# A whole decoder layer on eight cores: longest path first in the kernel's static scheduler, gated first transfers, and a first FFN group by token-block pairs

## The chip, the cores and the metric

The kernel runs on the 8 cores of one Trainium2 chip. Each core computes one sequence of the batch, with no traffic between cores. The metric is the device time of the slowest core, in microseconds (us). Most executions agree within 0.3%. In some executions one die (cores 0 to 3 or 4 to 7) gets a lower TensorE clock and the time is some per cent longer; those are called slow, and only fast runs are compared here.

## The reference, cut to what matters

One decoder layer on x (8, 2048, 1024) float32, with D = 1024 and a feed-forward width of 2816:

```python
x = x + 0.5 * swiglu(rmsnorm(x, ffn1_norm), w1, w3, w2)       # first FFN
h = rmsnorm(x, mix_norm)
u = h @ w_in                                                  # q, k, v, g_ret, x_lru, g_lru
ret   = retention_chunkwise(rotary(q), rotary(k), v)          # mixer A, 4 heads, 16 chunks of 128
y_ret = (silu(g_ret) * head_groupnorm(ret)) @ w_ret_o
xc    = causal_depthwise_conv(x_lru)                          # mixer B, 4 taps
r, i  = sigmoid(xc @ w_r + b_r), sigmoid(xc @ w_i + b_i)      # 8 blocks of 128 channels
a     = exp(-8 * r * softplus(-lam))
h_t   = a * h_{t-1} + sqrt(1 - a*a) * (i * xc)                # RG-LRU, a scan over time
y_lru = (h_t * gelu(g_lru)) @ w_lru_o
# ... sigmoid gates merge the two, then cross-attention on 256 memory tokens,
# the second FFN and the last rmsnorm
```

Retention and the RG-LRU (called the LRU from here) read the same `h` and do not depend on each other. The stretch of time in which both run is called the mixer.

## The kernel before

The kernel records every operation with what it reads and writes, its engine and a modelled cost. A scheduler in the same file then simulates the engines once, at build time, and fixes the order of every engine's queue. On the chip each queue runs in that order: an instruction whose data are late holds everything behind it on its engine (41.30 us of POOL in `norm_inline` below). So a modelled cost never delays anything on the chip by itself; it acts only by the order that it produces. Among the operations that its simulation holds to be ready, the scheduler takes the smallest `key`, and `key` is the place in the program.

```python
DMA_NS_PER_B = 1.0 / 300.0      # modelled DMA rate: 300 bytes per ns
DMA_LAT = 2000.0
TAB_NS = 1283.0                 # modelled load of an activation table
TAB_HOLD = 1200.0               # extra reluctance to change the table
...
        op.key = op.id if key is None else key     # program order
...
            if op.dma:
                s2 = max(end, dmafree[0])
                dmafree[0] = s2 + op.dma * DMA_NS_PER_B
                end = dmafree[0] + DMA_LAT         # when the scheduler believes the data have landed
```

The start: x comes as sixteen tiles of 128 tokens, each normalised (ACT square, POOL power, DVE scale), transposed by PE (8 small matmuls) and copied out. The FFN's weights come in blocks on another queue. All sixteen tiles stand in the program ahead of the first projection.

```python
    row = load_row("ffn1_norm", 0)
    consts_early()
    for tt in range(4):
        load_x(tt)
    f1.pump(3)                  # weight blocks
    for tt in range(4, 8):
        load_x(tt)
    f1.pump(6)
    for tt in range(8, 16):
        load_x(tt)
    for tt in range(16):
        norm_x(tt, row, bkT)    # normalise and transpose
    f1.pump()
    consts_late()
```

The mixer is recorded as sixteen LRU units (a channel block is two units, one for each half of the sequence) alternating with sixteen retention steps. One LRU unit, cut:

```python
            # PE: input projections -> ACT copies them to XL
            dve(...tensor_scalar(xc, XL, ...))                  # conv, then 3 scalar_tensor_tensor taps
            pool(...tensor_copy(xcb, xc))                       # XCB, bf16 for PE
            # PE: gate matmuls on XCB -> ACT: tanh -> TR, TI
            dve(...scalar_tensor_tensor(ti, ti, 1.0, xc, add, mult))
            act(mu, tr, Exp); act(tr, tr, Exp); act(mu, mu, Ln); act(mu, mu, Exp)
            pool(...tensor_tensor(mu, ti, mu, mult))
            dve(...tensor_tensor_scan(xc, tr, mu, ...))
            pool(...tensor_tensor(bt, xc, gg, mult))            # BT, the unit's output
```

Retention's matmuls use PSUM banks 2, 3 (projections q, k, v, gate: `bkp`), 5, 6, 7 (its memory work: `bkm`) and 4. Its output tile is `ATOK`.

The softmax here doesn't subtract the row's maximum and nothing guards it: scores larger than these inputs give would overflow.

Of the kernel before, what the change touches and what calls it, by code (L numbers as in the profile page):

```python
# [20 lines left out]
DMA_NS_PER_B = 1.0 / 300.0  # L21
DMA_LAT = 2000.0
TAB_NS = 1283.0
TAB_HOLD = 1200.0
# [11 lines left out]
class Op:  # L36
    __slots__ = ("eng", "fn", "id", "deps", "raw", "cost", "tab", "dma", "succ", "nd", "ready", "fin",
                 "pos", "marked", "idx", "sem", "semval", "prev", "clock", "key")


class Prog:
# [27 lines left out]
    def schedule(self):  # L69
# [5 lines left out]
        for op in ops:  # L75
            for d in op.deps:
                d.succ.append(op)
        pend = {e: [] for e in ENGS}
# [47 lines left out]
        while left:  # L126
# [36 lines left out]
            op.fin = end  # L163
            op.pos = len(order[se])
# [178 lines left out]
D = 1024  # L343
KC = 8
TB = 512
NTB = 4
# [47 lines left out]
def build(stage=None):  # L394
# [135 lines left out]
    def sp_dma(out, in_, reads, writes, nbytes):  # L530
        P.add("sp", lambda e: e.dma_start(out=out, in_=in_), reads=reads, writes=writes, cost=60, dma=nbytes)  # L531

    def wdma(out, in_, reads, writes, nbytes):
        P.add("pool", lambda e: e.dma_start(out=out, in_=in_), reads=reads, writes=writes, cost=900, dma=nbytes)  # L534
# [15 lines left out]
    def load_x(tt):  # L550
        v = xt(tt)
        sp_dma(v.ap, x_d[tt * 128:(tt + 1) * 128, :], [], v.hs, 128 * D * 4)
# [3 lines left out]
    def load_row(name, slot):  # L556
        v = ROW.v(slot * D, D)
        r = ROWIDX[name]
        sp_dma(v.ap, bass.AP(rows_d.tensor, r * D, [[0, 128], [1, D]]), [], v.hs, 128 * D * 4)
        return v  # L560
# [8 lines left out]
    def consts_late():  # L569
        dve(lambda e: e.memset(onesb.ap, 1.0), [], onesb.hs, 128)  # L570
        dve(lambda e: e.tensor_scalar(maskf.ap, io_i.ap, 0.0, None, ALU.is_ge), io_i.hs, maskf.hs, 128)
        sp_dma(pc.ap, prm_d, [], pc.hs, 128 * NPCOL * 4)
# [72 lines left out]
    def norm_T(src, row, j, dst_ap, dst_hs, bk):  # L645
# [19 lines left out]
        else:  # L665
            dve(lambda e: e.tensor_copy(dst_ap, src_v), [hbk[b]], dst_hs, D)
# [15 lines left out]
    class FFN:  # L682
# [6 lines left out]
        def pump(self, upto=NM):  # L689
            while True:  # L690
# [3 lines left out]
                if ok0 and (a <= b or not ok1):  # L694
                    v = W13.v((a % 9) * 2048, 2048)
                    wdma(v.ap, w13_d[self.which][a], [], v.hs, 128 * 2048 * 4)
                    self.nl[0] += 1
                elif ok1:
                    v = W2.v((b % 9) * 1024, 1024)
                    wdma(v.ap, w2_d[self.which][b], [], v.hs, 128 * 1024 * 4)  # L700
                    self.nl[1] += 1
# [40 lines left out]
        def run(self, bkp, bk2, post, side=None, pre=None):  # L742
            side = side or []
            pre = pre or (lambda tb: None)
            m0 = 0
            pend = None
            for g, G in enumerate(GROUPS):
                ms = list(range(m0, m0 + G))
                last = g == len(GROUPS) - 1
                for tb in range(NTB):  # L750
                    if g == 0:
                        pre(tb)
                    for gm, m in enumerate(ms):
                        self.w13(m, gm, tb, G, bkp)
                        if tb == NTB - 1:
# [4 lines left out]
                    if pend is not None:  # L760
                        pms, ptb, plast = pend
                        self.w2(pms, ptb, bk2, post if plast else None)
                        if ptb == NTB - 1:
                            self.used[1] += len(pms)
                            self.pump()
                    pend = (ms, tb, last)
                m0 += G
            pms, ptb, plast = pend
            self.w2(pms, ptb, bk2, post)
# [6 lines left out]
    def mem_jobs():  # L776
# [4 lines left out]
        def jn(mt):  # L781
            def f():
                if mt == 0:
                    row[0] = load_row("mem_norm", 1)
                s = MST.v(0, D)
                sp_dma(s.ap, mem_d[mt * 128:(mt + 1) * 128, :], [], s.hs, 128 * D * 4)
# [5 lines left out]
        def jproj(src_d, dst, fp):  # L792
            def f():
                b = bk_side.next()
                for j in range(2):
                    fc = 2 * fp + j
                    w = XW.v(j * D, KC, 128)
                    wdma(XW.v(j * D, D).ap, src_d[fc], [], w.hs, 128 * D * 4)
# [102 lines left out]
    def lru_units():  # L901
# [9 lines left out]
        def unit(u):  # L911
# [41 lines left out]
            dve(lambda e: e.scalar_tensor_tensor(ti.ap, ti.ap, 1.0, xc.ap, ALU.add, ALU.mult), ti.hs + xc.hs, ti.hs, 1024)  # L953
# [4 lines left out]
            pool(lambda e: e.tensor_tensor(mu.ap, ti.ap, mu.ap, ALU.mult), ti.hs + mu.hs, mu.hs, pool_cost(1024))  # L958
# [19 lines left out]
    def ret_steps():  # L978
        bkp = Banks([2, 3])
        bkm = Banks([5, 6, 7])  # L980
# [419 lines left out]
```

## Time and profile before

| | before |
|---|---|
| time, median of 4 runs (range; 2185.85 is a slow run) | 2070.54 us (2067.56 to 2185.85) |
| span of the profiled core | 2068.1 us |
| busy share PE, DVE, ACT, POOL | 86%, 44%, 30%, 19% |
| first conv of the LRU starts | 611.7 us |
| last retention output (ATOK) ends | 1016.9 us |
| last LRU output (BT) ends | 1201.3 us |
| from there to the end | 866.8 us |

Engines in the lines below: PE is the matmul engine, PEld its weight loads, DVE, ACT and POOL the vector, scalar and general engines.

The table of windows of the kernel before. Columns: window, its length, busy us of PE, PEld, DVE, ACT and POOL (instructions), granted PE clock, DMA share, GB/s.

```profile
core 5: us, PE busy (x) PEld busy (x) DVE busy (x) ACT busy (x) POOL busy (x), PEclk, DMA share, GB/s
...
40.00:60.00 20.00, 4.25 (x40) 3.25 (x40) 6.91 (x13) 7.99 (x15) 3.13 (x4) 0.56 1.03 232
60.00:80.00 20.00, 7.00 (x40) 4.15 (x40) 6.65 (x10) 5.78 (x10) 3.25 (x5) 0.59 0.99 206
...
612.00:1010.00 398.00, 309.75 (x1506) 142.71 (x1504) 259.44 (x426) 187.22 (x314) 166.25 (x124) 0.89 0.08 19
1010.00:1201.00 191.00, 90.97 (x323) 33.89 (x322) 71.03 (x55) 94.02 (x108) 52.72 (x32) 0.70 0.12 27
1201.00:2068.00 867.00, 850.02 (x4119) 388.80 (x4116) 325.43 (x469) 204.92 (x327) 101.66 (x143) 1.00 0.24 52
```

Three stretches can be seen. At the start PE hardly works while the DMA engines are full. From 1010 to 1201 us PE is busy less than half of the time, at a granted clock of 0.70. After 1201 us PE is busy 98% of the time.

The timeline of PE at the start. Columns: start, length, engine, line, operation, output and inputs, count; in brackets the idle time before it and what ended it.

```profile
36.80 1.89 PE L505 MATMUL bank<-hT,W_45 128*128 128x512 bf16 x8
...
51.60 1.01 PE L658 MATMUL bank<-identb,HB 128*128 128x128 bf16 x8 [9.57 <-DVE HB L650]
...
67.11 1.01 PE L658 MATMUL bank<-identb,HB 128*128 128x128 bf16 x8 [7.36 <-DVE HB L650]
...
73.94 3.16 PE L505 MATMUL bank<-hT,W_45 128*128 128x512 bf16 x8
84.51 1.01 PE L658 MATMUL bank<-identb,HB 128*128 128x128 bf16 x8 [7.41 <-DVE cst L590]
85.32 4.90 PE L505 MATMUL bank<-hT,W_45 128*128 128x512 bf16 x11
```

The rows with `identb` are transposes of x tiles, the rows with `W_45` projections. Between 38.7 and 73.9 us PE does no projection, although much of it could have run (`no_gates_no_pairs` below, whose loads land at nearly the same times, runs 64 matmuls from 30 us on): its queue has the transposes of the next tiles first, and those wait for x tiles that land one about every 4 us (the sixteen transfers land from 8.3 to 68.6 us). The last wait, of 7.41 us, is of the same kind but not for an x tile: ACT stood before the square of a memory tile (`MST`, for the cross-attention), and DVE's norm of the last x tile stood behind that. ACT's timeline:

```profile
81.06 1.06 ACT L521 ACTIVATE JUNK<-MST 128x1024 bf16<-128x1024 f32 x1 [8.07 <-DMA MST<-mem]
```

PE has finished only 24 projection matmuls when its steady work begins at 85.3 us.

The chain of waits of PE from 612 to 1183 us (what it waited for, us in total, times, longest), and three lines of POOL's timeline:

```profile
PE bank L505 <- POOL XCB L939: 62.8, 8, 20.4
PE bank L505 <- DVE T_87 L1000: 38.6, 15, 4.1
PE bank L505 <- ACT TI L521: 22.6, 8, 17.5
```

```profile
1015.47 1.45 POOL L1027 TENSOR_TENSOR ATOK<-RN,SG 128x512 bf16<-128x512 f32 x1
1032.98 2.36 POOL L966 TENSOR_TENSOR BT_73<-XC,GG 128x1024 bf16<-128x1024 f32 x1 [2.60 <-DVE XC L961]
1046.97 2.35 POOL L966 TENSOR_TENSOR BT_73<-XC,GG 128x1024 bf16<-128x1024 f32 x1 [2.60 <-DVE XC L963]
```

When the last retention output is written, only four of the eight LRU channels are done; BT_73 is the fifth. The other four run alone, and the wait for XCB, up to 20.4 us at a time, is PE waiting for the LRU's next conv with nothing else in hand.

### The profile page before, as it was taken

The numbers are of one execution on the slowest core, as the hardware profiler recorded it, in microseconds if no ns is written. First come the engines' busy times: TensorE is split into PE (matmuls) and PEld (weight loads), VectorE is DVE, ScalarE is ACT, GpSimd is POOL, SyncE is SP. The second block draws the span as 40 slices with busy tenths as digits, with TensorE's granted clock in tenths as the row PEclk, the third lists the DMA queues.
The fourth block names the chain that finished last, engine by engine and source line by source line (L and its number), as shares of the span: only waits on it lengthen the run. The fifth ranks groups of instructions, "written<-read, shape, count | busy, mean of one in ns | idle before, by whom it ended". The sixth has DMA issues, their size and how long they took to land.

```text
span 2068.1 us, 24090 instructions; the slowest of 8 cores (2053.9 to 2068.1 us)
## 1 busy us (share of the span) xinstructions
PE 1776.2 (86%) x8584; PEld 815.4 (39%) x8584; DVE 904.4 (44%) x1354; ACT 615.8 (30%) x964; POOL 395.7 (19%) x435
## 2 busy tenths in 40 slices
PE   2599999999988877777554499999999999999997
PEld 1244544444443333333221144444445444444443
DVE  3445223333576657565533321115555223333346
ACT  3311121111335353535444431113544111111122
POOL 4101101000124344444322232222001000000001
PEclk9699999999998989889766799999999999999999
DMA  9706557312551010000200052218202131031013
GB/s 221 158 13 93 73 89 117 67 25 32 129 146 24 9 31 11 21 20 12 72 11 0 11 82 41 41 31 219 62 1 33 30 61 32 1 61 31 11 46 123
DMA packets 39284, 118.51 MB, mean 57 GB/s; under 512 B 4480, under 2 KB 4480, under 8 KB 38912
## 3 DMA queue, kind: packets, MB, share of 16 engines
q0 software_dynamic: 23760, 64.50, 19.6%
q1 hardware_dynamic: 15408, 52.48, 7.5%
q8 instruction: 71, 1.16, 0.2%
q14 instruction: 45, 0.37, 0.1%
HBM read 158.38 MB, written 23.07 MB: 88 GB/s over the span
## 4 chain that ended last, share of the span: by engine, by line
PE 70%; DVE 8%; DMA 6%; ACT 6%; issue 5%; POOL 2%; SPq 2%; DVEq 0%; ACTq 0%; POOLq 0%
PE bank L505 68%; DMA MST<-mem 2%; SPq L531 2%; ACT MU L521 2%; DVE XC L936 1%; ACT TR L521 1%; DMA XW<-w_xo 1%; POOL MU L958 1%; ACT L521 1%; DVE XC L933 1%; DMA X<-park 1%; PE bank L658 1%; DVE XC L963 1%; DMA XW<-w_xqT 1%; DMA rope<-RT 1%
## 5 line engine op out<-in xcount | busy, mean ns | idle before, releaser
L505 PE MATMUL bank<-hT,W_45 128*128 128x512 bf16 x2816 | 626.4, 382 | 2.3 <-ACT STMP L521 2.3
L505 PEld LDWEIGHTS bank<-hT,W_45 128*128 128x128 bf16 x2816 | 277.0, 99 | 333.4 <-issue 12.5
L505 PE MATMUL bank<-W_46,HID 128*128 128x512 bf16 x1408 | 314.2, 379 | 3.2 <-DVE stat L641 1.8
L719 DVE TENSOR_TENSOR HID<-bank,STMP 128x512 bf16<-128x512 f32 x176 | 121.7, 691 | 440.8 <-PE bank L505 439.1
L521 ACT ACTIVATE STMP<-bank 128x512 f32<-128x512 f32 x176 | 104.8, 596 | 686.0 <-PE bank L505 685.9
L737 DVE SCALAR_TENSOR_TENSOR X<-bank,X 128x512 f32<-128x512 f32 x256 | 176.2, 691 | 111.6 <-PE bank L505 111.3
L505 PEld LDWEIGHTS bank<-W_46,HID 128*128 128x128 bf16 x1408 | 131.8, 97 | 174.2 <-issue 29.6
L505 PE MATMUL bank<-hT,LW 128*128 128x512 bf16 x512 | 128.1, 412 | 22.9 <-ACT TI L521 22.6
L521 ACT ACTIVATE JUNK<-X 128x1024 bf16<-128x1024 f32 x80 | 84.5, 1056 | 144.7 <-DVE X L737 57.6
L642 POOL TENSOR_TENSOR stat<-stat,cst 128x1 f32<-128x1 f32 x82 | 50.3, 614 | 376.2 <-DVE stat L641 368.7
L505 PE MATMUL bank<-hT,TW 128*128 128x512 bf16 x512 | 121.9, 382 | 0.0
L1187 DVE SCALAR_TENSOR_TENSOR TT_98<-TT_98,bank 128x512 f32<-128x512 f32 x64 | 43.9, 687 | 165.1 <-ACT TT_98 L521 164.9
L658 PE MATMUL bank<-identb,HB 128*128 128x128 bf16 x528 | 45.4, 236 | 72.7 <-DVE HB L650 51.4
L505 PE MATMUL bank<-XCB,wgate 128*128 128x512 bf16 x64 | 28.0, 485 | 86.9 <-POOL XCB L939 62.8
L521 ACT ACTIVATE TT_98<-bank,dcol 128x512 f32<-128x512 f32 x64 | 43.8, 687 | 166.4 <-PE bank L505 163.7
L505 PE MATMUL bank<-RW_76,hT 128*128 128x512 bf16 x256 | 72.3, 437 | 22.4 <-DVE T_87 L1000 13.5
L650 DVE SCALAR_TENSOR_TENSOR HB<-X,stat,ROW 128x1024 bf16<-128x1024 f32 x64 | 81.5, 1281 | 22.7 <-POOL stat L642 21.9
L505 PEld LDWEIGHTS bank<-hT,LW 128*128 128x128 bf16 x512 | 52.4, 104 | 96.1 <-issue 47.6
L505 PE MATMUL bank<-RW_75,hT 128*128 128x512 bf16 x256 | 69.4, 421 | 21.9 <-DVE T_87 L1000 10.4
L534 POOL DMA_DIRECT2D W_45<-f_w x44 | 24.4, 555 | 327.9 <-PE bank L505 327.4
L505 PEld LDWEIGHTS bank<-hT,TW 128*128 128x128 bf16 x512 | 50.4, 98 | 61.2 <-issue 1.6
L658 PEld LDWEIGHTS bank<-identb,HB 128*128 128x128 bf16 x528 | 37.3, 106 | 90.1 <-issue 81.0
(188 smaller groups left out, 2056.8 us busy)
## 6 DMA issues: line engine op xcount, KB each, us to landing
W_45<-f_w POOLq DMA_DIRECT2D x44, 512.0 KB, 8.9
W_46<-f_w POOLq DMA_DIRECT2D x44, 256.0 KB, 8.9
X<-x SPq DMA_DIRECT2D x16, 512.0 KB, 31.5
park<-X SPq DMA_DIRECT2D x16, 512.0 KB, 4.0
TW<-w_tail POOLq DMA_DIRECT2D x16, 512.0 KB, 6.9
X<-park SPq DMA_DIRECT2D x16, 512.0 KB, 18.3
out<-OST SPq DMA_DIRECT2D x16, 512.0 KB, 2.6
LW<-w_lru_in POOLq DMA_DIRECT2D x8, 512.0 KB, 5.3
```

The lines of the kernel that those rows point to most:

```text
L505: ins = e.matmul(out_ap, l, r, start=(start and i == 0), stop=(stop and i == n - 1), skip_group_check=skip)
L521: P.add("act", lambda e: e.activation(out, in_, func, **kw), reads=reads, writes=writes, cost=act_cost(n, nap), tab=tab)
L531: P.add("sp", lambda e: e.dma_start(out=out, in_=in_), reads=reads, writes=writes, cost=60, dma=nbytes)
L534: P.add("pool", lambda e: e.dma_start(out=out, in_=in_), reads=reads, writes=writes, cost=900, dma=nbytes)
L642: pool(lambda e: e.tensor_tensor(s[:, 2:3], s[:, 1:2], cc(2), ALU.pow), hs + cst.hs, hs, 550)
L650: dve(lambda e: e.scalar_tensor_tensor(hb.ap, src.ap, r, row.ap, ALU.mult, ALU.mult), src.hs + rh + row.hs, hb.hs, D)
L658: ins = e.transpose(bv[:, c * 128:(c + 1) * 128], hb.ap[:, c * 128:(c + 1) * 128], identb.ap)
L719: dve(lambda e: e.tensor_tensor(hd.ap, banks[b3][:, :], s.ap, ALU.mult), [hbk[b3]] + s.hs, hd.hs, TB)
L737: dve(lambda e, b=b, xv=xv: e.scalar_tensor_tensor(xv.ap, banks[b][:, :], 0.5, xv.ap, ALU.mult, ALU.add), [hbk[b]] + xv.hs, xv.hs, 512)
L933: dve(lambda e: e.tensor_scalar(xc.ap, XL.v(3, 1024).ap, pcol("conv_w", 24 + c), pcol("conv_b", c), ALU.mult, ALU.add), XL.v(3, 1024).hs + ...
L936: dve(lambda e, s=s: e.scalar_tensor_tensor(xc.ap, XL.v(s, 1024).ap, pcol("conv_w", s * 8 + c), xc.ap, ALU.mult, ALU.add), xl_all.hs + xc. ...
L1187: dve(lambda e, t=t, by=by: e.scalar_tensor_tensor(t.ap, t.ap, 1.0, banks[by][:, :], ALU.add, ALU.mult), t.hs + [hbk[by]], t.hs, TB)
```

## The change

The change has two aims: let the operation with the longest remaining path go first, and let the first transfers come in the order of use. The core of the diff, grouped by part, with cuts marked:

```diff
 # (1) scheduler's model: DMA slower and nearer the measured rate, table changes freer
-DMA_NS_PER_B = 1.0 / 300.0
-DMA_LAT = 2000.0
+DMA_NS_PER_B = 1.0 / 215.0
+DMA_LAT = 2500.0
-TAB_HOLD = 1200.0
+TAB_HOLD = 600.0
     # ... SP's modelled issue cost 60 -> 400, POOL's 900 -> 600, a PSUM copy 0.55 of its cost
 # (2) priority: longest path to the end
+        bl = {}
+        for op in reversed(ops):
+            m = 0.0
+            for x in op.succ:
+                if bl[x.id] > m:
+                    m = bl[x.id]
+            bl[op.id] = m + op.cost + (DMA_LAT if op.dma else 0.0)
+            op.key = -bl[op.id]
 # (3) gates: a transfer waits for an earlier one
-    for tt in range(4):
-        load_x(tt)
-    f1.pump(3)
     # ...
+    load_x(0)
+    wh = [f1.load13()]
+    load_x(1)
     # ...
+    wh.append(f1.load13(xt(1).hs))
+    for tt in range(4, 8):
+        load_x(tt, xt(0).hs)
     # ... and so on; x8 to x15 and all later weights and constants wait for weight blocks
 # (4) pairs: in the first group one weight block serves two token blocks
-                for tb in range(NTB):
+                for tbs in ([(0, 1), (2, 3)] if g == 0 else [(0,), (1,), (2,), (3,)]):
 # (5) LRU: the gated input goes back to XC, so TI is free earlier
-            dve(... scalar_tensor_tensor(ti.ap, ti.ap, 1.0, xc.ap, ALU.add, ALU.mult) ...)
+            dve(... scalar_tensor_tensor(xc.ap, ti.ap, 1.0, xc.ap, ALU.add, ALU.mult) ...)
 # (6) retention: one PSUM bank moves from its memory work to its projections
-        bkp = Banks([2, 3])
-        bkm = Banks([5, 6, 7])
+        bkp = Banks([2, 3, 7])
+        bkm = Banks([5, 6])
```

More of the change, by code (lines that the diff above doesn't have):

```diff
@@ L37 @@
     __slots__ = ("eng", "fn", "id", "deps", "raw", "cost", "tab", "dma", "succ", "nd", "ready", "fin",
-                 "pos", "marked", "idx", "sem", "semval", "prev", "clock", "key")
+                 "st", "pos", "marked", "idx", "sem", "semval", "prev", "clock", "key")
 class Prog:
@@ L163, in schedule @@
             op.fin = end
+            op.st = st
             op.pos = len(order[se])
@@ L530, in sp_dma @@
     def sp_dma(out, in_, reads, writes, nbytes):
-        P.add("sp", lambda e: e.dma_start(out=out, in_=in_), reads=reads, writes=writes, cost=60, dma=nbytes)
+        P.add("sp", lambda e: e.dma_start(out=out, in_=in_), reads=reads, writes=writes, cost=400, dma=nbytes)
     def wdma(out, in_, reads, writes, nbytes):
-        P.add("pool", lambda e: e.dma_start(out=out, in_=in_), reads=reads, writes=writes, cost=900, dma=nbytes)
+        P.add("pool", lambda e: e.dma_start(out=out, in_=in_), reads=reads, writes=writes, cost=600, dma=nbytes)
     def cc(i):
@@ L547, in dcol, with load_x, load_row @@
         return dc_.ap[:, base + i:base + i + 1]
-    def load_x(tt):
+    def load_x(tt, after=()):
         v = xt(tt)
-        sp_dma(v.ap, x_d[tt * 128:(tt + 1) * 128, :], [], v.hs, 128 * D * 4)
+        sp_dma(v.ap, x_d[tt * 128:(tt + 1) * 128, :], list(after), v.hs, 128 * D * 4)
     ROWIDX = {"ffn1_norm": 0, "mix_norm": 1, "xattn_norm": 2, "ffn2_norm": 3, "final_norm": 4, "mem_norm": 5}
-    def load_row(name, slot):
+    def load_row(name, slot, after=()):
         v = ROW.v(slot * D, D)
         r = ROWIDX[name]
-        sp_dma(v.ap, bass.AP(rows_d.tensor, r * D, [[0, 128], [1, D]]), [], v.hs, 128 * D * 4)
+        sp_dma(v.ap, bass.AP(rows_d.tensor, r * D, [[0, 128], [1, D]]), list(after), v.hs, 128 * D * 4)
         return v
@@ L567, in consts_early, with consts_late @@
             dve(lambda e, i=i, val=val: e.memset(cc(i), val), [], cst.hs, 1)
-    def consts_late():
+    def consts_late(gate):
         dve(lambda e: e.memset(onesb.ap, 1.0), [], onesb.hs, 128)
         dve(lambda e: e.tensor_scalar(maskf.ap, io_i.ap, 0.0, None, ALU.is_ge), io_i.hs, maskf.hs, 128)
-        sp_dma(pc.ap, prm_d, [], pc.hs, 128 * NPCOL * 4)
+        sp_dma(pc.ap, prm_d, gate, pc.hs, 128 * NPCOL * 4)
         pool(lambda e: e.iota(io_i.ap[:, 0:16], [[-128, 16]], base=1023, channel_multiplier=-1), [], io_i.hs, 400)
@@ L665, in norm_T @@
         else:
-            dve(lambda e: e.tensor_copy(dst_ap, src_v), [hbk[b]], dst_hs, D)
+            dve(lambda e: e.tensor_copy(dst_ap, src_v), [hbk[b]], dst_hs, D, 0.55)
     def norm_x(tt, row, bk):
@@ L687, in __init__, with load13, load2, pump @@
             self.st = 0
-        def pump(self, upto=NM):
+        def load13(self, after=()):
+            a = self.nl[0]
+            v = W13.v((a % 9) * 2048, 2048)
+            wdma(v.ap, w13_d[self.which][a], list(after), v.hs, 128 * 2048 * 4)
+            self.nl[0] += 1
+            return v.hs
+        def load2(self, after=()):
+            b = self.nl[1]
+            v = W2.v((b % 9) * 1024, 1024)
+            wdma(v.ap, w2_d[self.which][b], list(after), v.hs, 128 * 1024 * 4)
+            self.nl[1] += 1
+            return v.hs
+        def pump(self, upto=NM, gate=()):
             while True:
@@ L694, in pump @@
                 if ok0 and (a <= b or not ok1):
-                    v = W13.v((a % 9) * 2048, 2048)
-                    wdma(v.ap, w13_d[self.which][a], [], v.hs, 128 * 2048 * 4)
-                    self.nl[0] += 1
+                    self.load13(gate)
                 elif ok1:
-                    v = W2.v((b % 9) * 1024, 1024)
-                    wdma(v.ap, w2_d[self.which][b], [], v.hs, 128 * 1024 * 4)
-                    self.nl[1] += 1
+                    self.load2(gate)
                 else:
@@ L740, in w2, with run, flush @@
                     post(tt)
-        def run(self, bkp, bk2, post, side=None, pre=None):
+        def run(self, bkp, bk2, post, side=None):
             side = side or []
-            pre = pre or (lambda tb: None)
             m0 = 0
-            pend = None
+            pend = []
+            def flush(lst):
+                for a in lst:
+                    self.w2(*a)
+                    if a[1] == NTB - 1:
+                        self.used[1] += len(a[0])
+                        self.pump()
             for g, G in enumerate(GROUPS):
@@ L749, in run @@
                 last = g == len(GROUPS) - 1
-                for tb in range(NTB):
-                    if g == 0:
-                        pre(tb)
+                for tbs in ([(0, 1), (2, 3)] if g == 0 else [(0,), (1,), (2,), (3,)]):
+                    flush([a for a in pend if a[1] % 2 in [tb % 2 for tb in tbs]])
+                    pend = [a for a in pend if a[1] % 2 not in [tb % 2 for tb in tbs]]
                     for gm, m in enumerate(ms):
-                        self.w13(m, gm, tb, G, bkp)
-                        if tb == NTB - 1:
+                        for tb in tbs:
+                            self.w13(m, gm, tb, G, bkp)
+                        if tbs[-1] == NTB - 1:
                             self.used[0] += 1
@@ L759, in run @@
                             side.pop(0)()
-                    if pend is not None:
-                        pms, ptb, plast = pend
-                        self.w2(pms, ptb, bk2, post if plast else None)
-                        if ptb == NTB - 1:
-                            self.used[1] += len(pms)
-                            self.pump()
-                    pend = (ms, tb, last)
+                    flush(pend)
+                    pend = [(ms, tb, bk2, post if last else None) for tb in tbs]
                 m0 += G
-            pms, ptb, plast = pend
-            self.w2(pms, ptb, bk2, post)
+            flush(pend)
             while side:
@@ L774, in build, with mem_jobs @@
     bk_side = Banks([6, 7])
-    def mem_jobs():
+    def mem_jobs(gate):
         jobs = []
@@ L783, in f @@
                 if mt == 0:
-                    row[0] = load_row("mem_norm", 1)
+                    row[0] = load_row("mem_norm", 1, gate)
                 s = MST.v(0, D)
-                sp_dma(s.ap, mem_d[mt * 128:(mt + 1) * 128, :], [], s.hs, 128 * D * 4)
+                sp_dma(s.ap, mem_d[mt * 128:(mt + 1) * 128, :], gate, s.hs, 128 * D * 4)
                 norm_T(s, row[0], mt, mt_all.ap[:, :, mt * 128:(mt + 1) * 128], mt_all.hs, bk_side)
@@ L797, in f @@
                     w = XW.v(j * D, KC, 128)
-                    wdma(XW.v(j * D, D).ap, src_d[fc], [], w.hs, 128 * D * 4)
+                    wdma(XW.v(j * D, D).ap, src_d[fc], gate, w.hs, 128 * D * 4)
                     mm_group(banks[b][:, j * 256:(j + 1) * 256], b,
@@ L952, in unit @@
                         tab=S_TANH, bias=dcol(base, c), scale=0.5)
-            dve(lambda e: e.scalar_tensor_tensor(ti.ap, ti.ap, 1.0, xc.ap, ALU.add, ALU.mult), ti.hs + xc.hs, ti.hs, 1024)
+            dve(lambda e: e.scalar_tensor_tensor(xc.ap, ti.ap, 1.0, xc.ap, ALU.add, ALU.mult), ti.hs + xc.hs, xc.hs, 1024)
             act(mu.ap, tr.ap, AF.Exp, tr.hs + dc_.hs, mu.hs, 1024, tab=S_EXP, bias=dcol(8, c), scale=dcol(8, c))
@@ L957, in unit @@
             act(mu.ap, mu.ap, AF.Exp, mu.hs + cst.hs, mu.hs, 1024, tab=S_EXP, bias=cc(6), scale=0.5)
-            pool(lambda e: e.tensor_tensor(mu.ap, ti.ap, mu.ap, ALU.mult), ti.hs + mu.hs, mu.hs, pool_cost(1024))
+            pool(lambda e: e.tensor_tensor(mu.ap, xc.ap, mu.ap, ALU.mult), xc.hs + mu.hs, mu.hs, pool_cost(1024))
             prev = XC.v(((u + 1) % 2) * 1024 + 1023, 1)
@@ L1275, in build @@
     f1 = FFN(0)
+    consts_early()
+    load_x(0)
+    wh = [f1.load13()]
+    load_x(1)
     row = load_row("ffn1_norm", 0)
-    consts_early()
-    for tt in range(4):
-        load_x(tt)
-    f1.pump(3)
+    load_x(2)
+    load_x(3)
+    wh.append(f1.load13(xt(1).hs))
     for tt in range(4, 8):
-        load_x(tt)
-    f1.pump(6)
-    for tt in range(8, 16):
-        load_x(tt)
+        load_x(tt, xt(0).hs)
+    wh.append(f1.load13(xt(3).hs))
+    wh.append(f1.load13(xt(5).hs))
+    wh.append(f1.load13(wh[2]))
+    for tt in range(8, 12):
+        load_x(tt, wh[2])
+    wh.append(f1.load13(wh[3]))
+    for i in range(6):
+        f1.load2(wh[3] if i < 3 else wh[4])
+    for tt in range(12, 16):
+        load_x(tt, wh[4])
+    gate = wh[5]
     for tt in range(16):
         norm_x(tt, row, bkT)
-    f1.pump()
-    consts_late()
-    wdma(wgate.ap, wgate_d, [], wgate.hs, 128 * 2048 * 4)
+    f1.pump(gate=gate)
+    consts_late(gate)
+    wdma(wgate.ap, wgate_d, gate, wgate.hs, 128 * 2048 * 4)
     side = []
@@ L1294, in build @@
         side.append(lambda tb=tb: rope_piece(tb))
-    side = [lambda: None] * 2 + side + mem_jobs()
+    side = [lambda: None] * 2 + side + mem_jobs(gate)
     mixrow = [None]
@@ L1339, in build @@
     P.emit(nc)
+    build.prog = P
     return nc
```

## The prediction

> **What bounds it now.** The table of windows shows three stretches. (a) Start, 0 to 85 us: PE runs 16 tile transposes and 5 groups of the first projections; the DMA share is about 1.0 at some 220 GB/s until 80 us. The timeline shows x tiles landing every 4.1 us (the last at 68.7), because weights for nine blocks and side jobs share the queues, and ACT stuck behind a side-job tile until 81 us. (b) Mixer, 612 to 1201 us: DVE 331 us, ACT 281, POOL 219 busy in 589 us; none is full. Retention is done at about 1010 (24.9 us a step); the LRU then runs on alone for 190 us at about 53 us a channel, as a chain conv, cast, gates, four activations, multiply, scan, with PE's clock at 0.70. (c) 1201 to 2055: PE 100%, one 512-column matmul per 0.215 us. The change can hardly touch (c).
>
> **What the change does.** Start: gated transfers put x tiles and W13 blocks in order of use; a W13 block serves two token blocks (6.9 us of PE instead of 3.5). x0 to x3, row, two W13 blocks are 3.6 MB, 16 us at 220 GB/s; x4 to x7 and two blocks 3.1 MB more, 14 us; plus 2 us landing and 5.5 us norm chain (square 1.25, pow 0.55, scale 1.28, transposes 1.0, copy 1.0 and hops). The new order has eight tiles' transposes before the long run of projections, so PE runs steadily from about 38 us with 16 matmuls done (3.5 us). Before: 85 us with 40 done (8.6 us). Gain 76.4 - 34.5 = 42 us. x8 to x15 land by about 62 us, before PE asks (79 us).
>
> Mixer: the priority puts the LRU chain, the longest path, first. The changed order shows two retention steps for each LRU channel to the very end, not four and then none. It also frees TI earlier (result into XC), so the tanh of one unit goes before the exps of the one before. Work of one channel plus two steps, from durations of before: PE 41 us, DVE 41.5, ACT 36, POOL 24.5. The chain of a pair of units without competitor is some 35 to 40 us, with TI freed. With four engines at 60 to 75% and in-order queues I expect 55 us a channel: 8 x 55 + 10 = 450 us instead of 589, a gain of 139; some overlap with the tail is lost, so 130. The Trainium skill ("TensorE: Matmul & The Clock Gate", part 1) says an idle PE drops to half clock; the trace agrees (0.70 in the LRU-only stretch, 1.00 later), so denser work gives some back.
>
> Small: 5 us fewer gaps in the first FFN, 3 us at the end (the last PE run of second projections falls from 80 to 40 matmuls). Modelled costs matter only through the order. Work hardly changes: this is a reordering, all of it on critical stretches (a) and (b).
>
> **Sum.** 2072 - 42 - 130 - 8 = 1892; I say 1895 us, 1845 to 1950. Faster by over 2%: 0.95, same 0.04, slower 0.01.
>
> **What would show it.** Steady PE at 35 to 42 us; last projection of the first FFN near 550; scans of a channel every 52 to 58 us with retention outputs to the end; last BT product near 1020; PE busy share above 92%; tail to end unchanged (about 855 us).
>
> **What would make it wrong.** The static order comes from modelled costs: if the real engines differ (DVE slowed while POOL runs: the 0.82 us tensor_scalar took up to 2.93), a high-priority instruction blocks ready ones and a channel takes 65 to 70 us (total near 1990). Gates may serialize DMA and starve the start (gain 20 instead of 42). A finer chain could give 48 us a channel (1840).

## The result, and the profile after

Ratios here are the mean time of one kernel's fast runs over that of the other's fast runs of the same rounds, so they are not quite the ratio of the medians that are quoted.

| | before | after |
|---|---|---|
| time, median of 4 runs (range) | 2070.54 (2067.56 to 2185.85) | 1897.83 us (1896.65 to 1897.97) |
| ratio of fast runs (95% interval) | | 0.9169 (0.9151 to 0.9187) |
| span of the profiled core | 2068.1 | 1896.1 us |
| PE busy share | 86% | 91% |
| PE's steady work begins | 85.3 | 37.4 us |
| first conv of the LRU starts | 611.7 | 543.2 us |
| last retention output ends | 1016.9 | 1024.2 us |
| last LRU output ends | 1201.3 | 1029.0 us |
| from there to the end | 866.8 | 867.1 us |

So 68.5 us were gained before the first conv, 103.8 us in the mixer (589.6 us before, 485.8 after), and nothing behind it; the profiled spans differ by 172.0 us.

The table of windows after:

```profile
core 6: us, PE busy (x) PEld busy (x) DVE busy (x) ACT busy (x) POOL busy (x), PEclk, DMA share, GB/s
...
40.00:60.00 20.00, 19.89 (x92) 9.05 (x93) 5.56 (x10) 6.21 (x11) 2.70 (x5) 1.00 1.03 219
60.00:80.00 20.00, 17.38 (x102) 8.75 (x102) 8.42 (x13) 7.18 (x12) 5.36 (x10) 1.00 0.73 109
...
543.00:1029.00 486.00, 375.33 (x1859) 176.80 (x1894) 346.38 (x496) 276.24 (x427) 218.78 (x161) 0.89 0.13 28
1029.00:1896.00 867.00, 846.71 (x4038) 390.93 (x4117) 325.69 (x469) 203.25 (x327) 100.04 (x143) 0.99 0.24 55
```

From 40 to 60 us the DMA engines are as full as before, yet PE is busy 19.89 of 20 us instead of 4.25, and its clock is 1.00 instead of 0.56. PE's timeline at the start shows why: behind eight tiles' transposes stands one long row of projections.

```profile
36.94 0.61 PE L667 MATMUL bank<-identb,HB 128*128 128x128 bf16 x8 [1.69 <-DVE HB L659]
37.39 36.42 PE L514 MATMUL bank<-hT,W_45 128*128 128x512 bf16 x165
73.65 0.61 PE L667 MATMUL bank<-identb,HB 128*128 128x128 bf16 x8
```

PE's waits from 545 to 1005 us, and POOL's timeline at the end of the mixer:

```profile
PE bank L514 <- DVE SG L1088: 40.9, 9, 8.8
PE bank L1125 <- ACT AT_66 L530: 13.5, 3, 4.7
PE bank L1109 <- DVE RN L1045: 10.7, 6, 4.4
...
PE bank L514 <- DVE T_87 L1023: 8.2, 4, 5.2
...
PE bank L514 <- POOL XCB L962: 2.5, 1, 2.5
```

```profile
1022.93 1.28 POOL L1050 TENSOR_TENSOR ATOK<-RN,SG 128x512 bf16<-128x512 f32 x1
1026.69 2.35 POOL L989 TENSOR_TENSOR BT_68<-XC,GG 128x1024 bf16<-128x1024 f32 x1 [1.97 <-DVE XC L986]
```

The LRU no longer runs alone: retention ends 4.8 us before it, and the wait for XCB has fallen from 62.8 to 2.5 us. The largest wait is now for SG, the retention's gate. SG's tanh runs on ACT and needs another table than the LRU's Exp and Ln, so it stands behind them (ACT loads a table at 602.25 us, directly before SG's tanh).

### The profile page after: what moved, and what is told of

The parts are those of the page before. It is cut to its first block, busy times and chain, and to the rows that moved or that the text cites. A ratio compares the mean times of both kernels' runs of the same rounds, so it can differ in the third digit from the quotient of the medians.

```text
span 1896.1 us, 24126 instructions; the slowest of 8 cores (1883.6 to 1896.1 us)
## 1 busy us (share of the span) xinstructions
PE 1728.3 (91%) x8416; PEld 813.6 (43%) x8584; DVE 906.9 (48%) x1354; ACT 607.0 (32%) x964; POOL 388.3 (20%) x435
## 4 chain that ended last, share of the span: by engine, by line
PE 82%; DVE 6%; issue 5%; ACT 2%; DMA 2%; POOL 2%; DVEq 0%; SPq 0%; POOLq 0%; ACTq 0%
PE bank L514 79%; PE bank L667 1%; DVE XC L959 1%; DMA ROW<-rows 1%; POOL MU L981 1%; DMA TW<-w_tail 1%; ACT MU L530 1%; POOL rstat L1041 1%; DMA XW<-w_xo 1%; DVE rstat L1035 1%; DVE RN L1045 1%; DVE HB L659 1%; DVE rstat L1040 0%; DVE XC L986 0%; PE bank L1144 0%
## 5 line engine op out<-in xcount | busy, mean ns | idle before, releaser
L514 PE MATMUL bank<-W_46,HID 128*128 128x512 bf16 x1374 | 319.3, 380 | 5.0 <-DVE HID L738 2.1
L514 PEld LDWEIGHTS bank<-W_46,HID 128*128 128x128 bf16 x1408 | 136.1, 98 | 167.1 <-issue 12.2
L651 POOL TENSOR_TENSOR stat<-stat,cst 128x1 f32<-128x1 f32 x82 | 46.1, 564 | 361.7 <-DVE stat L650 361.6
L514 PE MATMUL bank<-hT,TW 128*128 128x512 bf16 x505 | 113.9, 379 | 3.7 <-DMA TW<-w_tail 1.8
L514 PE MATMUL bank<-hT,LW 128*128 128x512 bf16 x501 | 114.8, 382 | 1.3 <-ACT XL L530 0.4
L1214 POOL TENSOR_TENSOR MG<-TT_98 128x512 bf16<-128x512 f32 x32 | 40.5, 1266 | 158.2 <-DVE TT_98 L1210 147.0
L514 PE MATMUL bank<-RW_76,hT 128*128 128x512 bf16 x247 | 62.6, 397 | 8.0 <-DVE T_87 L1023 6.3
L514 PE MATMUL bank<-RW_75,hT 128*128 128x512 bf16 x250 | 62.7, 397 | 4.7 <-DVE T_87 L1023 1.9
L959 DVE SCALAR_TENSOR_TENSOR XC<-XL,pc,XC 128x1024 f32<-128x1024 f32 x48 | 62.2, 1296 | 2.0
```

Source lines behind the costliest of these rows:

```text
L514: ins = e.matmul(out_ap, l, r, start=(start and i == 0), stop=(stop and i == n - 1), skip_group_check=skip)
L651: pool(lambda e: e.tensor_tensor(s[:, 2:3], s[:, 1:2], cc(2), ALU.pow), hs + cst.hs, hs, 550)
L959: dve(lambda e, s=s: e.scalar_tensor_tensor(xc.ap, XL.v(s, 1024).ap, pcol("conv_w", s * 8 + c), xc.ap, ALU.mult, ALU.add), xl_all.hs + xc. ...
L1214: pool(lambda e, d=d, ts_=tuple(ts_): e.tensor_tensor(d.ap, ts_[0].ap, ts_[1].ap, ALU.add), ts_[0].hs + ts_[1].hs, d.hs, pool_cost(TB))
```

## The experiments

Twelve kernels were run; eleven were correct. They ran in four batches, each on one chip of its own with its own runs of the kernel before. Those of the first batch (four runs below, marked c1 in the table) were noisy: its fast runs of before spread from 2068.87 to 2096.95 us. So its ratios have wide intervals, and the milestones of the traces are the better witness.

For each, the mixer is split at one point of the trace: "both" runs from the first conv to the end of the last retention output, "alone" from there to the end of the last LRU output. All profiles in the table are of fast runs, and the rows are of the slowest core, but for `no_prio`. From core to core the mixer differs by a few us (481.3 to 485.8 us in the changed kernel), so differences of that size mean little.

Fast runs of one kernel spread by 22 to 28 us in three cases (`prio_only`, `no_prio`, `prio_dcost`); the profiled runs of the last two had a lower clock on some cores. In `prio_dcost` this cost time only behind the mixer (894.9 us from the last LRU output to the end on cores 4 and 5, 867.1 on undisturbed ones). In `no_prio` it fell into the mixer of the slowest core, core 4 (510.0 us, at a mean granted clock of 0.83 in "both" against 0.90 to 0.92 on cores 6 and 7), so its row is that of core 6, the slower mixer of the two undisturbed cores:

```profile
core 4: 1936.8 us, clock 0.944
core 6: 1913.1 us, clock 0.964
```

`no_pairs` was profiled only in the slow state and is left out of the table.

| run | median us (fast runs) | ratio (95%) | first conv | both | alone | mixer |
|---|---|---|---|---|---|---|
| before | 2069.14 (2067.56 to 2071.94) | 1 | 611.7 | 405.2 | 184.4 | 589.6 |
| `prio_only` c1 | 1996.13 (1994.81 to 2023.15) | 0.9633 (0.9406 to 0.9859) | 585.7 | 468.7 | 75.2 | 544.0 |
| `prio_dcost` | 1963.27 (1962.3 to 1984.62) | 0.9507 (0.9425 to 0.9589) | 544.7 | 467.6 | 75.6 | 543.2 |
| `banks_only` | 2033.5 (2028.98 to 2034.0) | 0.9808 (0.9763 to 0.9854) | 614.4 | 436.1 | 116.3 | 552.5 |
| `norm_inline` | 2076.91 (2074.33 to 2079.32) | 1.003 (1.0007 to 1.0053) | 619.0 | 403.2 | 185.3 | 588.5 |
| after | 1897.83 (1896.65 to 1897.97) | 0.9169 (0.9151 to 0.9187) | 543.2 | 481.0 | 4.8 | 485.8 |
| `no_prio` c1 (core 6) | 1938.39 (1919.12 to 1942.99) | 0.9268 (0.9122 to 0.9413) | 545.2 | 421.5 | 70.6 | 492.1 |
| `no_gates_no_pairs` c1 | 1894.23 (1893.39 to 1895.12) | 0.9079 (0.8997 to 0.9162) | 540.8 | 480.0 | 5.0 | 485.0 |
| `no_ti` | 1903.61 (1898.72 to 1903.7) | 0.9185 (0.9159 to 0.9211) | 545.9 | 474.6 | 18.9 | 493.5 |
| `no_banks` | 1938.15 (1934.01 to 1940.55) | 0.9366 (0.9335 to 0.9396) | 542.3 | 512.3 | 15.3 | 527.6 |
| `no_costs` | 1904.82 (1903.36 to 1907.16) | 0.92 (0.918 to 0.922) | 542.8 | 480.9 | 17.0 | 497.9 |
| `sg_copy` | 1902.27 (1899.8 to 1903.97) | 0.9179 (0.9127 to 0.923) | 543.2 | 422.9 | 66.7 | 489.6 |
| `mu2` | 1899.45 (1897.99 to 1900.76) | 0.9164 (0.9098 to 0.9229) | 542.6 | 484.7 | 4.6 | 489.3 |

Medians and ranges here are of the fast runs alone (the 2070.54 us above counts the slow run too).

### The start: is it the order of the transfers, or the order of the queues?

**`prio_only`: the kernel before with part (2) alone.**

```diff
         for op in ops: ...
+        # bl as in the change
+            op.key = -bl[op.id]
```

> The kernel before with the longest-path key alone, nothing else of the change. Theory: the priority carries nearly all of the mixer's gain (105 us of the 172), and does nothing for the start: about 1960 us (1940 to 1980), last product of the LRU some 490 to 510 us after the end of the first FFN. Rival: the freed TI buffer, the third projection bank and the new costs are needed for the mixer: 2000 to 2040 us.

The theory failed: the fast runs took 1994.81, 1996.13 and 2023.15 us, two just below the range of the rival and one inside it. Of the mixer's gain the priority brings 46 us. The first conv came 26 us earlier, but PE's steady work began only at 78.2 us; the other 19 us were gained later, in the first FFN. PE's timeline:

```profile
78.21 5.67 PE L513 MATMUL bank<-hT,W 128*128 128x512 bf16 x16
```

**`no_gates_no_pairs`: the change without parts (3) and (4).** The block of loads is the old one, and all four token blocks go singly.

```diff
-                for tbs in ([(0, 1), (2, 3)] if g == 0 else [(0,), (1,), (2,), (3,)]):
+                for tbs in [(0,), (1,), (2,), (3,)]:
-    load_x(0)
-    wh = [f1.load13()]
     # ... the old loads again, all gates empty
```

> The changed kernel with the old order of first transfers, no gates, and single token blocks in the first group of both FFNs. Theory: it loses the 43 us of the start and nothing else: 1935 to 1950 us, steady PE from 75 to 85 us. Rival: the priority by itself already puts the transfers in a good order: below 1915 us.

The rival held, and clearly: 1894.23 us, no slower than the change itself. The transfers came as slowly as before (the last x tile landed at 70.9 us, against 68.6 in the kernel before, 69.8 in `prio_only` and 60.7 in the change), and still PE ran steadily from 30 us:

```profile
27.81 1.01 PE L667 MATMUL bank<-identb,HB 128*128 128x128 bf16 x8 [4.64 <-DVE HB L659]
30.13 16.75 PE L514 MATMUL bank<-hT,W 128*128 128x512 bf16 x64 [1.31 <-DVE hT L675]
46.72 0.61 PE L667 MATMUL bank<-identb,HB 128*128 128x128 bf16 x8
```

Here PE's queue has 64 projection matmuls behind the first four tiles' transposes; before, it had 8 behind the first five. So neither the gates nor the pairs are needed for the gain at the start.

**`no_pairs`: the change without part (4).**

```diff
-                for tbs in ([(0, 1), (2, 3)] if g == 0 else [(0,), (1,), (2,), (3,)]):
+                for tbs in [(0,), (1,), (2,), (3,)]:
```

> The changed kernel with gates, but single token blocks in the first group. Theory: the gates do the work and the pairs save little, since the first blocks of weights are there when the first eight tiles are: 1898 to 1910 us. Rival: a block of weights for every 3.5 us of PE starves it: 1915 to 1935 us.

Three of its four runs fell into the slow state; the fast one took 1895.94 us. There is no ratio, and one fast run proves little. But in the profile the cores of die 0 were undisturbed (clock 0.969), and they agree with the change's cores: spans of 1887.0 to 1893.9 us (change: 1883.6 to 1896.1), first conv at 537.4 to 542.2 us (536.8 to 543.8). Nothing shows that the pairs save anything.

**`no_prio`: the change without part (2)**, so that everything goes in program order.

```diff
-            op.key = -bl[op.id]
```

> The changed kernel with program order as the key again, all else kept. Theory: the start keeps its 43 us, the mixer falls back to some 580 us: 2010 to 2035 us. Rival (buffers, banks and costs carry the mixer): 1920 to 1970 us.

The rival held: 1938.39 us. Of the three fast runs the shortest, 1919.12 us, is the one to compare, since the others had some cores at a lower clock; it lies 21 us above the change. The start stayed good (PE steady from 36.5 us), so with the gates and the new constants the priority is not needed there. In the mixer the LRU again ran 70.6 us alone, but the stretch of both was 60 us shorter than in the change, so the mixer is only about 6 us longer (492.1 and 489.1 us on the undisturbed cores, against 481.3 to 485.8). Of the rest, about 7 us lie before the first conv and 10 behind the mixer (876 us to the end, against 864 to 867).

**`norm_inline`: the kernel before, with each token block's tiles recorded just ahead of its projections.** This was to change PE's order and nothing else.

```diff
-    for tt in range(16):
-        norm_x(tt, row, bkT)
+    def pre1(tb):
+        for tt in range(4 * tb, 4 * tb + 4):
+            norm_x(tt, row, bkT)
-    f1.run(Banks([0, 1, 2, 3]), Banks([4, 5]), post1, side)
+    f1.run(Banks([0, 1, 2, 3]), Banks([4, 5]), post1, side, pre1)
```

> The kernel before, with one edit: the norms (and so the transposes) of a token block are recorded just before its own projections instead of all sixteen first. No gates, no pairs, no priority, old costs, transfers as before. The runs so far showed a steady start without any gate. Theory: what held PE until 85 us was the place of the sixteen transposes in its in-order queue, not the order of the transfers: PE steady from 25 to 35 us, 2020 to 2035 us against 2070. Rival: the transfers' order is needed: 2055 us or more.

The theory was not confirmed: 2076.91 us. The trace shows that the edit moved the block to another queue. POOL's timeline and PE's:

```profile
74.25 0.56 POOL L594 TENSOR_TENSOR cst<-cst 128x1 f32<-128x1 f32 x1 [41.30 <-DVE dcol L586]
75.21 5.22 POOL L642 TENSOR_TENSOR stat<-stat,cst 128x1 f32<-128x1 f32 x5 [0.40 <-DVE cst L596]
```

```profile
77.55 1.01 PE L658 MATMUL bank<-identb,HB 128*128 128x128 bf16 x8 [77.55 <-DVE HB L650]
```

POOL stood idle for 41.30 us before a power for the rotary constants. Its operand comes from DVE, and DVE stood behind other constants (`dcol`), whose parameters landed only at 71.8 us. The norms' powers (`stat`) stood behind it, and PE's first instruction came at 77.55 us. It is the same disease in another queue, but as a test of PE's order the run failed.

**`prio_dcost`: `prio_only` and, of part (1), the model of DMA alone.** No gates, no pairs, no bank split, no TI release.

```diff
-DMA_NS_PER_B = 1.0 / 300.0
-DMA_LAT = 2000.0
+DMA_NS_PER_B = 1.0 / 215.0
+DMA_LAT = 2500.0
     # and SP's modelled issue cost 60 -> 400
```

> The kernel before with the priority (longest path first) and only the scheduler's model of DMA made realistic (215 B per ns, 2500 ns latency, 400 ns an issue on SP): no gates, no pairs, no bank split, no TI release. Theory (the slow start is the order of the in-order engine queues, which the scheduler fixes from its modelled arrivals; the real order of transfers does not matter): the start is fixed without any gate, PE is steadily busy from 30 to 42 us of the span instead of about 80, and the time falls about 40 us under the priority alone (1994 to 2010 us): 1945 to 1970 us. Rival (the gates themselves are needed, since transfers share the bandwidth): PE steady only from 65 us or later and 1985 us or more.

The theory held in its core. The first conv came at 544.7 us, 41 us earlier than in `prio_only`, and two of the three fast runs took 1962.3 and 1963.27 us, inside the range; the third, 1984.62, had two cores at a lower clock. The edit costs the chip nothing and speeds no transfer: the last x tile landed at 71.1 us, later than the 69.8 of `prio_only`. What differs is the order of the queues. PE's timeline:

```profile
30.71 8.77 PE L513 MATMUL bank<-hT,W 128*128 128x512 bf16 x32 [1.43 <-DVE hT L674]
...
46.93 1.01 PE L666 MATMUL bank<-identb,HB 128*128 128x128 bf16 x8 [4.64 <-DVE stat L649]
47.84 26.01 PE L513 MATMUL bank<-hT,W 128*128 128x512 bf16 x112
```

Steady work in the strict sense begins at 47.8 us, later than the 30 to 42 that were expected, but 32 projection matmuls are done by then. The scheduler of the kernel before believed 300 bytes per ns, where the DMA engines moved 206 to 232 GB/s while full. So it counted on tiles that had not landed, and put their transposes ahead of projections that could have run. The run changed rate, latency and issue cost together; which of the three it takes was not tested, nor whether they help without the priority.

### The mixer: what brought the 104 us?

**`no_banks`: the change without part (6).**

```diff
-        bkp = Banks([2, 3, 7])
-        bkm = Banks([5, 6])
+        bkp = Banks([2, 3])
+        bkm = Banks([5, 6, 7])
```

> The changed kernel with two banks for the retention projections and three for the rest, as before. Theory (the two projection banks held retention at 25 us a step): a channel goes from 60 to 66 us, 1930 to 1950 us. Rival (LRU chain and table phases set the pace): below 1910 us.

The theory held: 1938.15 us, with a mixer 42 us longer than the change's. Of this, 31 us are in the stretch where both run. PE waits longer for the readers of the projection banks (T is the rotary product, SG the gate; 545 to 1045 us):

```profile
PE bank L514 <- DVE SG L1088: 43.1, 10, 8.3
PE bank L514 <- DVE T L1023: 24.6, 12, 5.0
PE bank L514 <- POOL XCB L962: 16.5, 8, 3.4
```

The line for T was 8.2 us in the changed kernel.

**`banks_only`: the kernel before with part (6) alone.**

```diff
-        bkp = Banks([2, 3])
-        bkm = Banks([5, 6, 7])
+        bkp = Banks([2, 3, 7])
+        bkm = Banks([5, 6])
```

> The kernel before with nothing but the bank split of the retention moved (three PSUM banks for its projections, two for its memory work), program order kept. Theory (the third projection bank lets retention's projections run ahead whatever the priority is): the mixer shortens by 30 to 55 us, from 590 us (first conv to end of the last gate matrix multiplication group) to 535 to 560; time 2015 to 2042 us, the start unchanged. Rival (the banks only pay when the priority feeds them, an interaction): mixer 575 us or more, time 2055 us or more.

The theory held: 2033.5 us, ratio 0.9808, a mixer of 552.5 us. The third projection bank is worth 37 us in the mixer even in program order, and the start is unchanged.

**`no_ti`: the change without part (5).**

```diff
-  ... scalar_tensor_tensor(xc.ap, ti.ap, 1.0, xc.ap, ALU.add, ALU.mult) ...
+  ... scalar_tensor_tensor(ti.ap, ti.ap, 1.0, xc.ap, ALU.add, ALU.mult) ...
-  ... tensor_tensor(mu.ap, xc.ap, mu.ap, ALU.mult) ...
+  ... tensor_tensor(mu.ap, ti.ap, mu.ap, ALU.mult) ...
```

> The changed kernel with the sum written back into TI, so that TI is held until the multiply on POOL. Theory (early release of TI is what lets the tanh of one unit go before the exps of the one before): a channel goes from 60 to 65 us, 1925 to 1945 us. Rival: the order makes up for it: below 1910 us.

The rival held: 1903.61 us, a mixer 8 us longer. The release of TI is worth little.

**`no_costs`: the change without part (1), all its constants.**

```diff
-DMA_NS_PER_B = 1.0 / 215.0
-DMA_LAT = 2500.0
-TAB_HOLD = 600.0
+DMA_NS_PER_B = 1.0 / 300.0
+DMA_LAT = 2000.0
+TAB_HOLD = 1200.0
     # and the old issue and copy costs
```

> The changed kernel with the scheduler's old constants (DMA rate and latency, table hold, issue costs, copy cost). Theory: the gates alone keep the start (the built order has eight tiles, then 160 projections), and the mixer changes by less than 10 us: 1890 to 1915 us. Rival: the old costs misplace the start or the table switches: above 1930 us.

The time is as expected, 1904.82 us. The start stays good, since gates are there too; the mixer is 12 us longer on the profiled core, a little more than the 10 expected, all of it the LRU alone at the end (489.2 to 497.9 us by core, against 481.3 to 485.8). With `prio_dcost` this shows two ways to a good start under the priority: gates, or a model of DMA nearer to the measured rate.

### What bounds the changed mixer?

**`sg_copy`: the change with retention's gate as a Copy instead of a Tanh**, which needs no table (in the changed kernel VS's Copies at 827.67 us stand between two Exps without a load). Its output is wrong, which doesn't matter for the time.

```diff
-            act(sg.ap, banks[outs[1]][:, :], AF.Tanh, [hbk[outs[1]]], sg.hs, 512, tab=S_TANH, scale=0.5)
+            act(sg.ap, banks[outs[1]][:, :], AF.Copy, [hbk[outs[1]]], sg.hs, 512, scale=0.5)
```

> The changed kernel with the retention gate's Tanh replaced by a Copy, which needs no table (wrong result on purpose; the same bytes and the same number of ACT instructions). Theory (in the changed mixer PE stands about 5 us per channel because the retention's projection banks wait for the gate Tanh that ACT holds back during the LRU's Exp and Ln phase): the channel shortens from 60 to 53 to 56 us and the time from 1897 to 1845 to 1870 us. Rival (the LRU's own chain, or the work of ACT and DVE, paces the channel, and PE's waits on the gate are only slack): within 1885 to 1905 us, channel 59 us or more.

The rival held: 1902.27 us. Retention did get faster, ending 58 us sooner after the first conv (422.9 us instead of 481.0). All of it was given back: the LRU then ran 66.7 us alone. PE's waits from 545 to 1005 us, and the moment in PE's timeline when retention has run out:

```profile
PE bank L514 <- POOL XCB L962: 34.4, 6, 26.0
...
PE bank L514 <- DVE SG L1088: 7.8, 3, 3.4
```

```profile
967.43 0.61 PE L1061 MATMUL bank<-identb,ATOK 128*128 128x128 bf16 x8
994.03 1.01 PE L514 MATMUL bank<-XCB,wgate 128*128 128x512 bf16 x2 [25.99 <-POOL XCB L962]
```

The wait for SG fell from 40.9 to 7.8 us and the wait for XCB rose from 2.5 to 34.4 us.

**`mu2`: the change with a second MU buffer for every other LRU unit of the first five channels.**

```diff
+    MU2 = A.buf("MU2", 60 * KB, F32, 1024)
-            mu = MU.v()
+            mu = (MU2 if u % 2 and u < 10 else MU).v()
```

> The changed kernel with a second MU buffer for the second half of each of the first five LRU channels (its place in memory is that of a gate output written only by the sixth), so that its exponentials need not wait until the first half's scan has read MU; the result stays right. In the changed kernel's trace the second half's first Exp starts at 832.53 us, just after the first half's scan, 830.14 to 832.43, though ACT was free for it some 5 us earlier. Theory (since the run with the gate Tanh replaced left the channel at 60 us, the LRU's own chain paces the mixer): 4 to 6 us less for each of five channels, 1868 to 1882 us. Rival (retention and the LRU bound the mixer together, retention ending only 9 us before the LRU, so shortening one alone moves nothing): 1888 to 1905 us, the last retention output still at 1005 us or later.

The rival held: 1899.45 us, the last retention output ending at 1027.3 us. In some channels both units' Exp and Ln now follow one another directly, as intended, yet the time does not move. PE's wait for SG fell from 40.9 to 28.0 us; another took its place:

```profile
PE bank L1111 <- DVE RN L1047: 31.4, 7, 13.0
```

RN is retention's normalised output, 10.7 us in the changed kernel. Shortening retention alone moved nothing, nor did this edit to the LRU's chain alone (that it made the chain shorter was meant, but is not shown: the mixer ran 489.3 us). A run with both at once, which would tell whether they then gain together, was not made; that stays open. No run beat the change by more than the 0.2% that `no_gates_no_pairs` shows, and that is between runs of different batches, so it counts as level.

## Why the prediction was right or wrong

The total was right: 1895 us predicted, 1897.83 measured. That it came so near was partly luck: some of its parts were wrong, and they offset each other, too much for the mixer and too little for the first FFN.

- **Start, "Gain 76.4 - 34.5 = 42 us": the size about right, the cause wrong.** Steady work began at 37.4 us (38 predicted) instead of 85.3. The prediction took 40 matmuls as done by 85 us, where the trace has 24; with 24 before and 15 after, at its 0.215 us each, the gain is 47.9 - 1.9 = 46 us. But it put the gain down to gated transfers "in order of use". They did what it said of them (the eighth x tile landed at 30.1 us, the last at 60.7), but they were not needed. `no_gates_no_pairs` has neither gates nor pairs and a start as good; `prio_dcost` gets 41 us from constants of a model. The gain is that PE's queue holds projections where it held transposes of tiles not yet landed.
- **"Modelled costs matter only through the order": right, and undervalued.** That was set aside as small. At the start the order is the whole effect.
- **First FFN, "5 us fewer gaps": too small.** From steady PE to the last matmul of the first FFN, 522.1 us (85.3 to 607.4) became 503.2 (37.4 to 540.6), 19 us less. In those windows PE's idle time fell from 20.8 to 10.6 us. The windows have nearly equal numbers of weight loads (2472 and 2474), though not quite of the same work (16 and 18 tiles' transposes); the other 9 us I did not resolve. The priority alone is enough to close the gaps: in `prio_only` this stretch took 504.0 us (78.2 to 582.2) with 9.4 us idle. It isn't the only way, since `no_prio` took 506.5 us without it.
- **Mixer, "55 us a channel": the step that failed.** It took 60.2 us a channel (BT_69's second output at 605.2 us to BT_68's at 1026.7, over seven channels), and the gain was 104 us instead of 130. The prediction credited the priority and the release of TI, and never mentioned the bank split. Taking a part away costs in the mixer: banks 42 us, all the constants 12, TI 8, priority about 6. Adding one alone to the kernel before gives: priority 46, banks 37. These don't add up to 104 in either direction, since the parts overlap, and most of all the priority: 46 us by itself, about 6 where the others are there. The bank split keeps its worth either way.
- **What the priority does: right in kind.** It said that retention would last to the end beside the LRU. It does: 4.8 us of the LRU alone instead of 184.4. But the priority alone pays for it: in `prio_only` the LRU alone shrank by 109 us while the stretch of both grew by 63, from 405.2 to 468.7, presumably because retention's instructions now stand behind the LRU's. The third bank takes much of that back: 512.3 us of both without it, 481.0 with it. And beside the other parts the priority's trade is nearly even: 421.5 us of both and 70.6 alone without it (`no_prio`), 481.0 and 4.8 with it.
- **PE "above 92%": missed slightly**, 91%. It follows from the 60 us a channel.
- **Clock: right.** The Trainium skill ("TensorE: Matmul & The Clock Gate", Part 1) says that PE's clock is cut to half when it has been little busy. This agrees: 0.70 on average in the stretch where the LRU ran alone, 0.56 at the starved start, 1.00 where PE is full. After the change no stretch of the mixer of 60 us is below 0.86.
- **Tail "unchanged": right** in that nothing changed, 866.8 and 867.1 us, where about 855 was named; so the "3 us at the end" were not there either.

In one sentence: a good total here was the sum of a start of the right size, a mixer overestimated by 26 us, and a first FFN underestimated by 14 us, and the bank split that carried a large part of the mixer was not seen.

Two chains bound the changed mixer together: retention and the LRU end 4.8 us apart, and both experiments that aimed to relieve one of them moved no time. That is shown for these two edits. Why a channel takes 60 us rather than 55 is not settled beyond it: the wait for SG was a true wait of retention, but not the limit of the mixer.

## What to carry to other kernels

Where a static scheduler fills in-order queues, look at the order behind the first late transfer before reordering transfers: here a modelled rate that was too high put waiting work ahead of ready work, and correcting three constants of the model did, under the priority, what a set of gates does. When a change bundles several edits, take each away and also add it alone, because a small unnamed edit (here one PSUM bank) may carry more than the headline; a part that gives much alone may give little beside the others, and only both tests show it. Compare undisturbed cores when you do so: the slowest core of `no_prio` would have made the priority's share 24 us instead of 6. When two independent chains share the engines, split the stretch into "both" and "one alone": a gain in one chain that comes back as time of the other alone is no gain.

## What the Trainium skill lacked or had wrong

- "ScalarE: Activation LUTs", section "What ACT_TABLE_LOAD costs", states about 1283 ns for the load plus about 1380 ns of drain, 2.66 us a switch. The load agrees (27 loads of 1283 ns in the changed kernel), the drain does not show: after each of the 27 the next ACTIVATE starts 1.29 to 1.30 us after the load's start. A load starting at 784.55 us, where the ACTIVATE before it ends, is followed by one at 785.85 us. ACT's timeline of the changed kernel:

```profile
783.95 0.60 ACT L530 ACTIVATE SB<-bank 128x512 bf16<-128x512 f32 x1 [1.68 <-PE bank L1155]
784.55 1.28 ACT L530 ACT_TABLE_LOAD   x1
785.85 1.08 ACT L530 ACTIVATE GG<-bank 128x512 f32<-128x512 f32 x2
```

- "GPSIMD Engine Reference", section "1. Specifications", says that its memory interface is shared with VectorE, with contention for some DVE modes. That section has no size for it; the lock behind it is treated elsewhere in the skill, so this is a gap of the section only. The conv's first DVE instruction took 0.81 us (at 805.45 us) with POOL idle and 2.80 us beside POOL's product (at 785.27 us), so a POOL instruction of 2.34 us can cost the DVE nearly 2 us. Of the sixteen in the changed kernel, the seven beside such a product took 2.54 to 2.93 us:

```profile
785.17 2.34 POOL L989 TENSOR_TENSOR BT_72<-XC,GG 128x1024 bf16<-128x1024 f32 x1 [2.60 <-DVE XC L986]
785.27 2.80 DVE L956 TENSOR_SCALAR XC<-XL,pc 128x1024 f32<-128x1024 f32 x1
...
805.45 0.81 DVE L956 TENSOR_SCALAR XC<-XL,pc 128x1024 f32<-128x1024 f32 x1 [1.21 <-ACT XL L530]
```

- "Trainium Architecture — The Big Picture", section "Inside one NeuronCore", says that every engine has its own instruction stream and that streams meet only at semaphores. The section lacks what follows from it for a kernel with in-order queues: one late operand holds all ready work behind it on that engine. Here that cost 41.30 us of POOL in one stroke (`norm_inline`), and some 46 us of PE at the start of the kernel before.
